# Convolution items, late gate operations and the split of w_out given lower scheduling rank in a hybrid encoder layer

## The chip, the core and the metric

The kernel runs on one core of one Trainium2 chip. The metric is the device time of one execution, in microseconds, as the median of several runs. The engines are TensorE (PE, with its weight loads shown as PEld), VectorE (DVE), ScalarE (ACT), GpSimd (POOL) and SyncE (SP), which issues the DMA transfers. Each engine executes its own list of instructions strictly in order, and waits on semaphores of the others.

## The reference

One layer of a hybrid encoder is applied to two requests with shared weights: a prompt of 512 tokens and a sample of 1024 tokens, model width 1024.

```python
h = rmsnorm(x, norm_attn_g);  z = h @ w_in
q, k, v, ca, cb = split(z)                     # 512, 128, 128, 512, 512 columns
a_out = window_attn(q, k, v, bias, sink)       # 8 heads of 64, 2 kv heads, |q-k| <= 128
c = ca * sigmoid(cb)
c = dwconv(c, conv_dw_w, 31 taps) + conv_dw_b
c = silu(layernorm(c, conv_ln_g, conv_ln_b))
x = x + concat(a_out, c) @ w_out
h = rmsnorm(x, norm_ffn_g)
u = dwconv(h @ w_up, ffn_dw_w, 3 taps) + ffn_dw_b   # 2 x 2816 columns
x = x + (silu(u[:, :2816]) * u[:, 2816:]) @ w_down
y = rmsnorm(x, norm_final_g)
```

All of it is float32.

## The kernel before

**Arithmetic.** A float32 product is emulated by three matmuls in the faster fp32r type. `split()` makes the two halves of an operand: the high half is a cast on ACT (L189), the low half is the subtraction of that cast from the original, on POOL or DVE (L190). A product of a 128-row chunk is then high x high, high x low, low x high, into one PSUM bank.

**Stages.** Work is cut into blocks of 128 tokens: blocks 0 to 3 are the prompt, 4 to 11 the sample.
1. The input projection (L296 to L299 in `proj()`), the prompt's attention and its output projection, to about 393 us.
2. The prompt's FFN up-projection in `ffn_step(k)`, 22 steps. A step makes a gate half and a value half with `up_half()`: 24 matmuls by `proj()` into a PSUM bank `u`, then the evacuation of the bank by ACT (L841) into a tile of the SBUF class `h`, with two taps of the 3-tap convolution read from the same bank by DVE (L837). The bank is free after the taps. `gate()` then makes tanh on ACT into a bank `b` (L861), two products on DVE and POOL (L866, L867), and the store of the result to DRAM (`gt`, L868). Beside these steps run the sample's attention (units 8 to 23, one for each block and kv head: `scores()`, then `values()`) and the sample's 31-tap convolution (`conv_items()`), whose result goes through DRAM (`cvd`).
3. The sample's output projection, from about 683 to 788 us. For each block `conv_norm()` loads the convolution's rows (L669), transposes them on PE (L675), makes the layer norm's statistics on DVE (L678, L681), transposes back (L687), applies scale and bias on ACT (four L690), tanh (L692), a product on DVE (L693) and a cast on ACT (L694). `out_half()` multiplies: matmuls L711, L712 and L713, 24 for each half block, of which the first twelve read the attention's rows and the last twelve the convolution's. Beside it run `pair_sums()` over the stored gates (on POOL, stores L883) and the first transposes of the sample's FFN input (`turned()`, L987).
4. The sample's FFN, whose order of instructions is written out by hand (the place `manual_schedule` in the program), to the end at 1557 us.

**The end of an attention unit.** `values()` ends with a copy of the result to a tile of class `h` (L638), a cast (L639), a subtraction on DVE (L640) and, on POOL, the sum L642 that frees both tiles.

**What sets the order.** In stages 1 to 3 the program is written once, in a certain order, and a scheduler lists the instructions of each engine: it plays the program through with estimated times, and among instructions that are ready takes the one with the lowest priority number (`tc.cur_priority`, which counts up as the program is written). So an instruction with a raised number yields to those that are written later, as long as they are ready. The place in the writing is set by three queues. `side` holds the generators of attention, w_out's split and conv_norm, and `tick()`, which `proj()` and `up_mm()` call as they go, advances it by `pace["rate"]` (RD in the FFN steps, RN after the attention). `convs` and `late` hold the generators of the convolution for the prompt and the sample. SBUF tiles come from fixed classes of slots (`q`, `c`, `h`, `d`, `s`; `h` has 61 slots of 2048 bytes per partition), handed out in the program by the class `Slots`; a tile that gets a used slot waits for the last reader of the tile before. PSUM banks are `a` (3), `u` (2), `b` (2) and `c` (1).

**w_out's split.** After attention unit 23, `sample()` goes through 16 + WOA pieces: each loads a piece of w_out (1024 rows as 8 x 128, in two halves of 512 columns) and, five pieces later, splits one (L189, L190).

Of the kernel before, what the change touches and what calls it, by code (L numbers as in the profile page):

```python
# [36 lines left out]

RA, RB, RBO, RD, RN, RE = 1.2, 0.8, 2.5, 0.8, 0.95, 0.9  # L40


CA, CB = 0.9, 0.4
# [10 lines left out]
OB = "uc"  # L54
VG = 3
NW = 36
KEEP = 3
U0 = 2


# [82 lines left out]
def tile_hybrid_encoder(ctx: ExitStack, tc: tile.TileContext, xs, rel_bias, norm_attn_g, w_in,  # L143
# [9 lines left out]

    sb = Slots(big, dict(q=(15, 4096), c=(4, 4224), h=(61, 2048), d=(2, 2176), s=(32, 64)), "q", KEEP)
    banks = Slots(lambda tag: ps[two_of[tag]], dict(a=(3, 2048), u=(2, 2048), b=(2, 2048), c=(1, 2048)))
    use = dict(step="aub", turn="aub", conv="c", attn="au", norm="b", out="b", up="u", down="b")
# [4 lines left out]
    def bank(job):  # L161
        return banks.tile([NT], among=use[job])
# [51 lines left out]
    def rows_T(parts, out):  # L214
        r = sb.tile([P])
        n = 0
        for src, k in parts:
            nc.sync.dma_start(r[n:n + k, :], src)
            n += k
        pt = bank("step")  # L220
        nc.tensor.transpose(pt[:, :n], r[:n, :], ident[:n, :n])
        nc.vector.tensor_copy(out, pt[:, :n])
# [3 lines left out]
    rows_T([(rw(norm_attn_g), 8)], vecs[:, 0:8])  # L226
    for _ in range(NW // 4):
        pt = bank("step")
# [36 lines left out]
    side, pace = deque(), dict(rate=0.0, due=0.0, conv=0.0, credit=0.0, late=0.0)  # L265

    def advance(queue):
        try:
            return next(queue[0])
        except StopIteration:  # L270
            queue.popleft()
            return 0.0
# [15 lines left out]
    def drain(queue):  # L288
        while queue:
            advance(queue)  # L290
# [21 lines left out]

    convs, late = deque(), deque()

    def conv_items(g, c, cp):
        T = GR[g]["T"]
        w = lambda t: cvw[:, t * 4 + c:t * 4 + c + 1]
        cost = 0.13 + NT / 960.0
        noff = NOFF[g]
        off = list(range(CK - noff, CK))  # L320
        for n in range(T // NT):
            src = lambda t: cp[:, t + n * NT:t + (n + 1) * NT]
            pacc = sb.tile([NT])

            def offload(k):
                t = off[k]
                if k == 0:
                    nc.scalar.activation(pacc[:], src(t), AF.Identity, scale=w(t))
                else:
                    pr = sb.tile([NT])  # L330
                    nc.scalar.activation(pr[:], src(t), AF.Identity, scale=w(t))
                    nc.gpsimd.tensor_tensor(pacc[:], pacc[:], pr[:], op=ALU.add)

            acc = bank("conv")
            nc.vector.tensor_scalar(acc[:], src(0), w(0), cvb[:, c:c + 1], op0=ALU.mult, op1=ALU.add)
            yield cost
            k = 0
            for t in range(1, CK - noff):
                nc.vector.scalar_tensor_tensor(acc[:], src(t), w(t), acc[:], op0=ALU.mult, op1=ALU.add)  # L339
                if t % 2 == 1 and k < noff:  # L340
                    offload(k)
                    k += 1
                yield cost
            while k < noff:
                offload(k)
                k += 1
            nc.vector.tensor_tensor(pacc[:], acc[:], pacc[:], op=ALU.add)
            del acc
            nc.sync.dma_start(cvd[g][:, c, n * NT:(n + 1) * NT], pacc[:])
            yield cost  # L350

    tanh_t, cpads, kt, vt = {}, {}, {}, {}
# [77 lines left out]
    def step(i, nt):  # L430
        kind, c, col = order[i]
        pp = bank("step")
        proj(pp[:], ws[i], h1[nt], i < 2 and nt == 0)
        evac(kind, c, nt, pp[:])
        if kind == "ca" and nt != 1:
            g = 0 if nt == 0 else 1
            (convs, late)[g].append(conv_items(g, c, cpads.pop((g, c))))
        tick()

    want_raw(1)  # L440
# [62 lines left out]
    bias = []  # L503
# [13 lines left out]
    qt, cats, units = {}, {}, {}  # L517
# [13 lines left out]
    score_rows = []  # L531

    def sink_columns():
        for h in range(0, NH, 2):
            t = sb.tile([2, NT])
            for n in range(2):
                nc.vector.tensor_copy(t[:, n, 0:1], nsink[:, h + n:h + n + 1])
            score_rows.append(t)
# [110 lines left out]
    def attention(u0, u1, then={}):  # L649
        yield from scores(u0)  # L650
        for u in range(u0, u1):
            if u + 1 < u1:
                yield from scores(u + 1)
            yield from values(u)
            if u in then:
                yield from then[u]
# [83 lines left out]
    def split_wo(kc, n, dve=False):  # L740
        wo[kc, n] = split(wor.pop((kc, n)), dve)
# [52 lines left out]
    def want_up_raw(k, half):  # L794
        if k < len(seq):
            upr[k, half] = chunk_raw(w_up[0], half * FF + seq[k][1] * P)
# [18 lines left out]
    def want_up(k, half):  # L815
        if k < len(seq):
            upw[k, half] = split(upr.pop((k, half)))
# [41 lines left out]
    def gate(j, a, b):  # L859
        th, t = bank("gate"), sb.tile([NT])  # L860
        nc.scalar.activation(th[:], a[:], AF.Tanh, scale=0.5)  # L861
        if j % 4 == VG:
            nc.vector.scalar_tensor_tensor(th[:], th[:], 1.0, a[:], op0=ALU.add, op1=ALU.mult)
            nc.vector.tensor_tensor(t[:], th[:], b[:], op=ALU.mult)
        else:
            nc.vector.scalar_tensor_tensor(t[:], th[:], 1.0, a[:], op0=ALU.add, op1=ALU.mult)  # L866
            nc.gpsimd.tensor_tensor(t[:], t[:], b[:], op=ALU.mult)  # L867
        nc.sync.dma_start(gt[j][:], t[:])  # L868
# [17 lines left out]
    def ffn_step(k):  # L886
        want_up_raw(k + 1, 1)
        ug = up_half(k, 0)
        want_up(k + 1, 0)
        uv = up_half(k, 1)  # L890
        want_up_raw(k + 2, 0)
        want_up(k + 1, 1)
        gate(k, ug[0], uv[0])

    use.update(attn="ab", gate="b")
    for half in range(2):
        want_up(0, half)
    want_up_raw(1, 0)
    load_bias()
    def sample():  # L900
        sink_columns()
        yield from attention(8, 24)
        kt.clear(), vt.clear(), qt.clear(), bias.clear(), score_rows.clear()
        use.update(norm="a")
        pace.update(rate=RN)
        for m in range(16 + WOA):
            if m in (10, 12):
                load_cat(m // 2 - 1)
            if m < 16:
                load_wo(m // 2, m % 2)  # L910
            if m >= WOA:
                split_wo((m - WOA) // 2, m % 2, m % 4 < DW2)
                yield 0.0
        drain(late)
        for m in range(NE):
            yield from conv_norm(4 + m)

    pace.update(rate=RD, late=CD)
    for k in range(NJ):
        if k == U0:  # L920
            side.append(sample())
        ffn_step(k)
# [320 lines left out]
    for j in range(2):  # L1243
        st[j] = dict(x=wide())
        prod(st[j]["x"][:, L], j, 1, True, True)
        a = sb.tile([NT])
# [322 lines left out]
    u, e, o11, o12 = (acc.pop(n) for n in ("u", "e", "o11", "o12"))  # L1569
# [73 lines left out]
```

## Time and profile before

| | |
|---|---|
| runs | 1566.2, 1563.84, 1559.77 us; median 1563.84 |
| profiled execution | 1558.91 us, its span 1557.1 us, granted clock 0.99 |
| PE busy | 1506.9 us (97%), 6843 instructions |
| DVE, ACT, POOL busy | 1126.2 (72%), 795.4 (51%), 708.9 us (46%) |
| DMA | 227.17 MB, mean 146 GB/s |
| 0 to 393 us | PE busy 367.0 of 393.0 us |
| 393 to 683 us (prompt's FFN, sample's attention) | PE busy 285.67 of 290.00 us |
| 683 to 788 us (sample's output projection) | PE busy 99.93 of 105.00 us |
| 788 us to the end (sample's FFN) | PE busy 754.29 of 769.00 us |

Starts and durations in the timeline's rows are in microseconds. A row names the engine, the line of the program, the operation, the tile written and the tiles read, and behind them in brackets how long the engine was idle just before, with the instruction whose end released it. Matmuls are pipelined, so their busy times overlap and the distance of two starts says how fast they go. The column PEclk is the clock granted to PE, as a share of the full one.

### The profile page before, as it was taken

The numbers are of one execution on the slowest core, as the hardware profiler recorded it, in microseconds if no ns is written. First come the engines' busy times: TensorE is split into PE (matmuls) and PEld (weight loads), VectorE is DVE, ScalarE is ACT, GpSimd is POOL, SyncE is SP. The second block draws the span as 40 slices with busy tenths as digits, with TensorE's granted clock in tenths as the row PEclk, the third lists the DMA queues.
The fourth block names the chain that finished last, engine by engine and source line by source line (L and its number), as shares of the span: only waits on it lengthen the run. The fifth ranks groups of instructions, "written<-read, shape, count | busy, mean of one in ns | idle before, by whom it ended". The sixth has DMA issues, their size and how long they took to land. (4 is left out here: it accounts for less than half of the span.)

```text
span 1557.1 us, 20112 instructions
## 1 busy us (share of the span) xinstructions
PE 1506.9 (97%) x6843; PEld 1229.4 (79%) x6843; DVE 1126.2 (72%) x1604; ACT 795.4 (51%) x1404; POOL 708.9 (46%) x566
## 2 busy tenths in 40 slices
PE   8899998999999999899999999999999999999997
PEld 6787787787888888777777888888888788888885
DVE  7999767857788785344868777777776845568883
ACT  4634654335787786633454444455545543444254
POOL 7652344226666776947433455555554000003355
PEclk9999999999999999999999999999999999999999
DMA  7582334447343346779332233333331582356644
GB/s 230 156 212 81 107 100 124 129 142 217 112 132 129 118 129 181 242 238 298 114 93 76 92 104 104 105 104 102 102 115 64 200 284 82 105 165 230 221 135 162
DMA packets 228780, 227.17 MB, mean 146 GB/s; under 512 B 13268, under 2 KB 168348, under 8 KB 228549
## 3 DMA queue, kind: packets, MB, share of 16 engines
q1 hardware_dynamic: 228677, 225.88, 45.8%
q8 instruction: 54, 0.88, 0.2%
q14 instruction: 49, 0.40, 0.1%
HBM read 164.74 MB, written 62.14 MB: 146 GB/s over the span
## 5 line engine op out<-in xcount | busy, mean ns | idle before, releaser
L190 POOL TENSOR_TENSOR q<-q,q 128x1024 fp32r<-128x1024 f32 x72 | 173.4, 2415 | 93.4 <-ACT q L189 34.4
L940 POOL TENSOR_TENSOR q<-q,q 128x512 fp32r<-128x512 f32 x101 | 140.0, 1391 | 164.0 <-ACT q L1050 151.7
L940 DVE TENSOR_TENSOR h<-h,h 128x512 fp32r<-128x512 f32 (+2 forms) x202 | 153.9, 794 | 65.2 <-ACT h L944 25.3
L1398 PE MATMUL w<-h,h 128*128 128x512 f32 x462 | 181.4, 393 | 1.4 <-DVE q L1185 1.4
L1399 PE MATMUL w<-h,h 128*128 128x512 f32 x462 | 181.5, 393 | 0.0
L1400 PE MATMUL w<-h,h 128*128 128x512 f32 x462 | 181.1, 392 | 0.0
L1064 PE MATMUL w<-h,q 128*128 128x512 f32 x448 | 176.5, 394 | 1.0 <-ACT h L1147 0.6
L1066 PE MATMUL w<-h,q 128*128 128x512 f32 x448 | 175.5, 392 | 1.0 <-POOL q L940 1.0
L1065 PE MATMUL w<-h,q 128*128 128x512 f32 x426 | 166.4, 391 | 0.0
L296 PE MATMUL u<-h,q 128*128 128x512 f32 x400 | 161.0, 403 | 5.4 <-DVE h L837 4.1
L297 PE MATMUL u<-h,q 128*128 128x512 f32 x400 | 158.6, 397 | 0.0
L299 PE MATMUL u<-h,q 128*128 128x512 f32 x384 | 151.8, 395 | 2.7 <-POOL q L190 2.7
L937 POOL TENSOR_TENSOR q<-q,q 128x1024 f32<-128x1024 f32 x12 | 32.4, 2707 | 236.6 <-DVE q L937 220.0
L339 DVE SCALAR_TENSOR_TENSOR c<-c,cvw,c 128x512 f32<-128x512 f32 x184 | 138.0, 750 | 2.9
L944 ACT CAST h<-h 128x512 fp32r<-128x512 f32 x120 | 71.9, 619 | 93.2 <-DVE h L940 41.9
L296 PE MATMUL b<-h,q 128*128 128x512 f32 x256 | 102.7, 401 | 3.3 <-DVE d L369 2.2
L1398 PEld LDWEIGHTS w<-h,h 128*128 128x128 f32 x462 | 86.8, 188 | 21.6 <-ACT h L944 1.8
L1400 PEld LDWEIGHTS w<-h,h 128*128 128x128 f32 x462 | 86.7, 188 | 19.7
L1399 PEld LDWEIGHTS w<-h,h 128*128 128x128 f32 x462 | 86.8, 188 | 19.5
L837 DVE SCALAR_TENSOR_TENSOR h<-u,fw,h 128x511 f32<-128x511 f32 x88 | 65.5, 744 | 49.8 <-ACT h L841 49.0
L299 PE MATMUL b<-h,q 128*128 128x512 f32 x256 | 101.4, 396 | 0.0
L297 PE MATMUL b<-h,q 128*128 128x512 f32 x256 | 101.1, 395 | 0.0
(417 smaller groups left out, 3670.4 us busy)
## 6 DMA issues: line engine op xcount, KB each, us to landing
q<-in_w_up SPq DMA_DIRECT2D x88, 512.0 KB
ga<-q SPq DMA_DIRECT2D x64, 256.0 KB
h<-ga SPq DMA_DIRECT2D x57, 256.0 KB
q<-in_w_in SPq DMA_DIRECT2D x28, 512.0 KB
h<-in_w_down SPq DMA_DIRECT2D x52, 256.0 KB
q<-in_x_sample SPq DMA_DIRECT2D x15, 512.0 KB
h<-qsd SPq DMA_DIRECT2D x24, 256.0 KB
x1d<-q SPq DMA_DIRECT2D x11, 512.0 KB
```

What stands on the lines that cost most here:

```text
L190: (nc.vector if dve else nc.gpsimd).tensor_tensor(lo[:], raw[:], hi[:].bitcast(F32), op=ALU.subtract)
L296: nc.tensor.matmul(out, whi[:, kc, :], hi[:], start=(kc == 0), stop=False)
L297: nc.tensor.matmul(out, whi[:, kc, :], lo[:], start=False, stop=False)
L299: nc.tensor.matmul(out, wlo[:, kc, :], hi[:], start=False, stop=(kc == KC - 1))
L339: nc.vector.scalar_tensor_tensor(acc[:], src(t), w(t), acc[:], op0=ALU.mult, op1=ALU.add)
L940: (eng or nc.vector).tensor_tensor(out, a, b, op=ALU.subtract)
L1064: nc.tensor.matmul(out, whi[:, s], hi[:], start=(start and c == 0), stop=False, **go)
L1065: nc.tensor.matmul(out, whi[:, s], lo[:], start=False, stop=False, **go)
L1066: nc.tensor.matmul(out, wlo[:, s], hi[:], start=False, stop=(stop and c == 3), **go)
L1398: nc.tensor.matmul(out, sh[:, c], th[:], start=(p == 0), stop=False)
L1399: nc.tensor.matmul(out, sh[:, c], tl[:], start=False, stop=False)
L1400: nc.tensor.matmul(out, sl[:, c], th[:], start=False, stop=(p == NPAIR - 1))
```

## The change

Five edits, none of which adds or removes an instruction; the number of instructions of each engine is the same as before.

1. RD, the pace of the side queue in the FFN steps, goes from 0.8 to 0.84, and RN, its pace after the attention, from 0.95 to 0.9.
2. A new wrapper `behind(gen, n)` raises the priority number by n while a generator writes its instructions. The convolution's generators get +200 (prompt) and +1500 (sample).
3. The instructions of `gate()` get +60.
4. The pieces of w_out become a generator of their own, `wo_pieces()`, with +150.
5. Two of these pieces are written after each of the attention units 19 to 23, and what is left of them after the last unit, as before.

```diff
--- before.py
+++ after.py
@@ -37,7 +37,7 @@
 
 
 
-RA, RB, RBO, RD, RN, RE = 1.2, 0.8, 2.5, 0.8, 0.95, 0.9
+RA, RB, RBO, RD, RN, RE = 1.2, 0.8, 2.5, 0.84, 0.9, 0.9
 
 
 CA, CB = 0.9, 0.4
@@ -54,7 +54,12 @@
 OB = "uc"
 VG = 3
 NW = 36
+WOU = 19
 KEEP = 3
+
+
+BACK = (200, 1500)
+BACKW, BACKG = 150, 60
 U0 = 2
 
 
@@ -311,6 +316,18 @@
     rs2 = cst.tile([P, 12], F32, name="rs2")
 
     convs, late = deque(), deque()
+
+    def behind(gen, n):
+
+        while True:
+            tc.cur_priority += n
+            try:
+                cost = next(gen)
+            except StopIteration:
+                return
+            finally:
+                tc.cur_priority -= n
+            yield cost
 
     def conv_items(g, c, cp):
         T = GR[g]["T"]
@@ -434,7 +451,7 @@
         evac(kind, c, nt, pp[:])
         if kind == "ca" and nt != 1:
             g = 0 if nt == 0 else 1
-            (convs, late)[g].append(conv_items(g, c, cpads.pop((g, c))))
+            (convs, late)[g].append(behind(conv_items(g, c, cpads.pop((g, c))), BACK[g]))
         tick()
 
     want_raw(1)
@@ -890,19 +907,16 @@
         uv = up_half(k, 1)
         want_up_raw(k + 2, 0)
         want_up(k + 1, 1)
+        tc.cur_priority += BACKG
         gate(k, ug[0], uv[0])
+        tc.cur_priority -= BACKG
 
     use.update(attn="ab", gate="b")
     for half in range(2):
         want_up(0, half)
     want_up_raw(1, 0)
     load_bias()
-    def sample():
-        sink_columns()
-        yield from attention(8, 24)
-        kt.clear(), vt.clear(), qt.clear(), bias.clear(), score_rows.clear()
-        use.update(norm="a")
-        pace.update(rate=RN)
+    def wo_pieces():
         for m in range(16 + WOA):
             if m in (10, 12):
                 load_cat(m // 2 - 1)
@@ -911,6 +925,21 @@
             if m >= WOA:
                 split_wo((m - WOA) // 2, m % 2, m % 4 < DW2)
                 yield 0.0
+
+    def some(gen, n):
+        for _ in range(n):
+            if next(gen, None) is None:
+                return
+            yield 0.0
+
+    def sample():
+        sink_columns()
+        wos = behind(wo_pieces(), BACKW)
+        yield from attention(8, 24, {u: some(wos, 2) for u in range(WOU, 24)})
+        kt.clear(), vt.clear(), qt.clear(), bias.clear(), score_rows.clear()
+        use.update(norm="a")
+        pace.update(rate=RN)
+        yield from wos
         drain(late)
         for m in range(NE):
             yield from conv_norm(4 + m)
```

The lines behind the first edits are shifted in the new program: by 5 up to `tick()` (L189 becomes L194, L296 becomes L301), by 17 from `conv_items()` on (L638 becomes L655, L642 becomes L659, L675 becomes L692, L687 becomes L704, L711 to L713 become L728 to L730, L841 becomes L858, L861 becomes L878), and by 29 behind `sample()` (L987 becomes L1016). On every engine the order is the same in both programs up to 393 us, and PE's again from 788 us on. In between it differs in many places; three of them follow. In the rows a tile stands as class and slot, the running number of the tile, and the instruction that wrote it.

First place, ACT near the end of the attention (645 to 654 us before). Here u_362 and u_363 are the two banks of step 19, one for the gate half and one for the value half. Before:

```order
L638 COPY h53_978_6332<-b0_360_6315 64x512
L639 CAST h24_957_6202<-b0_360_6315 64x512
L189 CAST q1_1024_6502<-q5_985_6362 128x1024
L189 CAST q12_1004_6435<-q0_981_6350 128x1024
L189 CAST h33_1042_6576<-h22_1028_6521 128x512
L841 ACTIVATE h46_1003_6431<-u0_362_6364,vecs_84,fw_275 128x512
L189 CAST h41_1052_6627<-h17_1031_6533 128x512
L189 CAST h31_1035_6547<-h24_1014_6474 128x512
L861 ACTIVATE b1_364_6506<-h46_1003_6431 128x512
L189 CAST h2_1012_6464<-h0_990_6383 128x512
L841 ACTIVATE h45_1022_6496<-u1_363_6439,vecs_84,fw_275 128x512
```

ACT of the change, from the evacuation of u_363 on, with the copy of the last attention unit (b0_360) in its middle:

```order
L635 CAST h40_1007_6388<-b1_358_6383 128x512
L858 ACTIVATE h19_1035_6522<-u1_363_6477,vecs_84,fw_275 128x512
L878 ACTIVATE b1_361_6418<-h32_996_6340 128x512
L655 COPY h32_1017_6449<-b0_360_6407 64x512
L656 CAST h48_982_6266<-b0_360_6407 64x512
L194 CAST q9_1023_6473<-q10_1012_6412 128x1024
L194 CAST h48_1020_6465<-h46_965_6180 128x512
L858 ACTIVATE h40_1022_6469<-u0_362_6426,vecs_84,fw_275 128x512
L878 ACTIVATE b1_364_6532<-h40_1022_6469 128x512
```

The evacuation of u_363 now stands ahead of that of u_362, and the latter, into slot h40, behind the copy of the last attention unit. The same place on POOL of the change, where slot h40 is read by the unit's last sum:

```order
L195 TENSOR_TENSOR h44_1006_6374<-h40_897_5788,h41_1005_6373 128x512
L195 TENSOR_TENSOR q1_1049_6582<-q3_1036_6526,q6_1048_6581 128x1024
L884 TENSOR_TENSOR q12_1015_6419<-q12_1015_6419,q9_1011_6408 128x512
L659 TENSOR_TENSOR h47_983_6267<-h40_1018_6450,h32_1017_6449 64x512
L195 TENSOR_TENSOR q0_1024_6474<-q10_1012_6412,q9_1023_6473 128x1024
```

The tile h40_1018 is the subtraction's result of the last unit, and h40_1022 of the rows above takes its slot.

Second place, PE in the output projection, block 6. The tile a_376 is the transpose of the block's convolution rows, a_377 the transpose back. Before:

```order
L675 MATMUL a2_376_6773<-ident_75,h56_1079_6767 128x128 x4
L711 MATMUL c0_375_6758<-h27_1032_6535,h24_1054_6637 128x512
L712 MATMUL c0_375_6758<-h58_1033_6536,h24_1054_6637 128x512
L711 MATMUL u0_378_6835<-h19_1029_6523,h24_1054_6637 128x512
L712 MATMUL u0_378_6835<-h16_1030_6524,h24_1054_6637 128x512
L713 MATMUL c0_375_6758<-h27_1032_6535,h4_1055_6638 128x512
```

PE of the change:

```order
L692 MATMUL a0_376_6773<-ident_75,h16_1079_6767 128x128 x4
L1016 MATMUL b0_392_7321<-ident_75,q12_1133_7042 128x128
L1016 MATMUL b1_393_7336<-ident_75,q12_1133_7042 128x128
L704 MATMUL a1_377_6793<-ident_75,h15_1085_6785 128x128 x4
L692 MATMUL a1_384_7061<-ident_75,h18_1137_7055 128x128 x4
L728 MATMUL u0_383_7046<-h49_1026_6486,h19_1077_6765 128x512
L729 MATMUL u0_383_7046<-h50_1027_6487,h19_1077_6765 128x512
L728 MATMUL u1_386_7123<-h48_1020_6465,h19_1077_6765 128x512
L729 MATMUL u1_386_7123<-h32_1021_6466,h19_1077_6765 128x512
```

Before, output matmuls of block 5 follow the transpose L675, and the transpose back stands 32 PE instructions later; in the change two single transposes stand between the two, and behind the transpose back one more transpose ahead of the matmuls that read the block's convolution rows (h19_1077). On SP, the load of block 6's convolution rows stands 11 instructions behind block 5's before, and 40 behind it in the change, after the loads and stores of the pair sums.

Third place, PE in block 7 of the change; a_381 and a_385 are the transposes back of blocks 7 and 8, c_387 is an output bank of block 7:

```order
L704 MATMUL a0_381_6934<-ident_75,h8_1112_6926 128x128 x4
L704 MATMUL a2_385_7081<-ident_75,h38_1143_7073 128x128 x4
L730 MATMUL u1_391_7308<-h26_971_6198,h47_1139_7058 128x512
L728 MATMUL u1_391_7308<-h41_1005_6373,h10_1138_7057 128x512
L729 MATMUL u1_391_7308<-h44_1006_6374,h10_1138_7057 128x512
L730 MATMUL u1_391_7308<-h41_1005_6373,h47_1139_7058 128x512
L1016 MATMUL b0_392_7321<-ident_75,q9_1160_7183 128x128
L1016 MATMUL b1_393_7336<-ident_75,q9_1160_7183 128x128
L728 MATMUL c0_387_7187<-h49_1026_6486,h16_1104_6906 128x512
```

Before, the transpose back of block 8 stands among the matmuls of c_387 that read attention rows (h10_1111, h12_1112), and the first with convolution rows (h9_1108) follows them:

```order
L711 MATMUL c0_387_7187<-h47_1001_6427,h10_1111_6916 128x512
L687 MATMUL a1_385_7081<-ident_75,h24_1143_7073 128x128 x4
L712 MATMUL c0_387_7187<-h1_1002_6428,h10_1111_6916 128x512
L713 MATMUL c0_387_7187<-h47_1001_6427,h12_1112_6917 128x512
L711 MATMUL c0_387_7187<-h2_1012_6464,h10_1111_6916 128x512
L712 MATMUL c0_387_7187<-h25_1013_6465,h10_1111_6916 128x512
L713 MATMUL c0_387_7187<-h2_1012_6464,h12_1112_6917 128x512
L711 MATMUL c0_387_7187<-h26_1020_6492,h10_1111_6916 128x512
L712 MATMUL c0_387_7187<-h28_1021_6493,h10_1111_6916 128x512
L713 MATMUL c0_387_7187<-h26_1020_6492,h12_1112_6917 128x512
L711 MATMUL c0_387_7187<-h27_1032_6535,h9_1108_6912 128x512
```

The transposes back of the two blocks now follow each other directly, and eight instructions behind the first stands the first matmul of c_387 with the convolution rows of block 7 (h16_1104).

## The prediction

> **What bounds the kernel now.** I read the page first, then the busy time by stage, then TensorE's timeline in the stages where it is not full, and last the other engines' timelines at the same moments.
>
> ```profile
> span 1557.1 us, 20112 instructions
> PE 1506.9 (97%) x6843; PEld 1229.4 (79%) x6843; DVE 1126.2 (72%) x1604; ACT 795.4 (51%) x1404; POOL 708.9 (46%) x566
> ```
>
> TensorE (PE) is the bound: 50 us of the span are left without a matmul. The change moves no matmul in or out, so the time can move only by what PE waits and by the clock that it is granted after a wait. Up to 393 us and from 788 us on, PE's order is the same in both programs; between them stand the 22 steps of the prompt's FFN with the sample's attention, and the sample's output projection.
>
> ```profile
> 393.00:640.00 247.00, 247.00 (x1199) 206.84 (x1198) 190.00 (x372) 188.59 (x358) 170.98 (x106) 1.00 0.45 141
> 640.00:655.00 15.00, 11.66 (x50) 8.93 (x48) 5.29 (x8) 10.66 (x17) 14.84 (x10) 1.00 0.86 268
> 655.00:663.00 8.00, 7.25 (x25) 5.85 (x26) 1.29 (x2) 0.00 (x0) 8.00 (x7) 0.79 0.39 132
> 684.00:690.00 6.00, 5.05 (x17) 4.09 (x18) 4.79 (x8) 2.69 (x5) 5.83 (x9) 0.72 1.03 364
> 690.00:730.00 40.00, 40.00 (x188) 32.78 (x188) 16.91 (x25) 14.56 (x31) 29.47 (x45) 1.00 0.87 288
> 730.00:750.00 20.00, 16.87 (x82) 13.16 (x81) 10.77 (x15) 6.80 (x14) 10.75 (x15) 1.00 0.81 264
> ```
>
> Columns: stretch, length, then busy us (and count) of PE, PEld, DVE, ACT, POOL, then the clock. From 393 to 640 us PE is never idle. It loses time at three places only: 640 to 663, 682 to 690, and 730 to 750. What it loses there is the most that can be won, and the clock column (0.79, 0.72) says that a wait costs more than itself.
>
> ```profile
> 650.32 0.40 PE L711 MATMUL c<-h,h 128*128 128x512 f32 x1
> 650.55 0.40 PE L712 MATMUL c<-h,h 128*128 128x512 f32 x1
> 651.59 0.47 PE L296 MATMUL u<-h,q 128*128 128x512 f32 x1 [0.64 <-DVE h L837]
> 651.90 0.40 PE L297 MATMUL u<-h,q 128*128 128x512 f32 x1
> 655.75 0.76 PE L296 MATMUL u<-h,q 128*128 128x512 f32 x1 [3.45 <-DVE h L837]
> 656.31 0.63 PE L297 MATMUL u<-h,q 128*128 128x512 f32 x1
> ...
> 658.87 0.41 PE L297 MATMUL u<-h,q 128*128 128x512 f32 x1
> ...
> 682.16 0.60 PE L675 MATMUL a<-ident,h 128*128 128x128 f32 x4
> 684.95 0.47 PE L711 MATMUL u<-h,h 128*128 128x512 f32 x1 [2.19 <-DVE s L678]
> ...
> 686.56 0.63 PE L711 MATMUL u<-h,h 128*128 128x512 f32 x1
> ...
> 689.12 0.85 PE L675 MATMUL a<-ident,h 128*128 128x128 f32 x4
> ```
>
> ```profile
> 734.11 0.66 PE L675 MATMUL a<-ident,h 128*128 128x128 f32 x4 [1.45 <-DMA h<-cvd]
> ...
> 744.29 0.44 PE L987 MATMUL b<-ident,q 128*128 128x128 f32 x2 [1.00 <-DVE q L958]
> ...
> 745.64 0.63 PE L687 MATMUL a<-ident,h 128*128 128x128 f32 x4 [0.67 <-DVE h L681]
> ```
>
> Starts are the clean measure, because matmuls overlap: at full clock one starts each 0.23 us (656.31 less 655.75 is already slow; 650.55 follows its neighbour by 0.23). First place: 1.04 - 0.23 = 0.81, then 3.85 - 0.23 = 3.62, then seven matmuls from 655.75 to 658.87 in 3.12 instead of 1.61, so 1.5: 5.9 us. Second: 2.79 less four transposes of 0.11 is 2.35, and six matmuls from 686.56 to 689.12 cost 2.56 instead of 1.38, so 1.2: 3.5 us. Third: 1.45 + 1.00 + 0.67 idle, by starts some 0.17 more each: 3.6 us. **13.0 us** in all.
>
> The first place is what the change speaks of. ACT takes its instructions in order:
>
> ```profile
> 651.70 0.62 ACT L189 CAST h<-h 128x512 fp32r<-128x512 f32 x1 [1.32 <-DMA h<-in_w_out]
> ...
> 653.26 0.77 ACT L841 ACTIVATE h<-u,vecs,fw 128x512 f32<-128x512 f32 x1
> 654.07 1.53 DVE L837 SCALAR_TENSOR_TENSOR h<-u,fw,h 128x511 f32<-128x511 f32 x2 [0.52 <-ACT h L841]
> 657.39 8.79 POOL L190 TENSOR_TENSOR h<-h,h 128x512 fp32r<-128x512 f32 x7
> ```
>
> The cast of a late w_out piece (L189) stands ahead of the evacuation of an FFN bank (L841); the taps (L837) follow, and only then may PE write the bank again at 655.75. POOL does w_out's low halves (1.26 us each) without a break until 666.
>
> **The change, part by part.** *Rates* (RD 0.84, RN 0.9) and *conv_items behind all else*: no instruction more or less; they shift units of the attention and the taps of the convolution against the FFN. In 393 to 640 DVE, ACT and POOL have 57, 58 and 76 us free, which hides any such shift; where the cover is gone, a late L837 costs PE one for one. I take 0, bounds -0.5 and +3 (TensorE was never idle there, so there is next to nothing to win).
>
> *The gate 60 later*: L861 to L868 come later; their results are read only after the FFN, so the delay itself is hidden. But the gate's inputs stay in SBUF longer, and the next step's tiles wait for slots. And its stores (L868) stand on SP ahead of loads of w_up.
>
> *w_out's split*: 48 loads on SP, 16 splits (0.62 on ACT, 1.26 on POOL each: 10 and 20 us) start some three FFN steps earlier. They are hidden behind PE there, by the same free time. What I then looked for is what comes last at the three places. With the casts spread, the wait at 655.75 for a w_out piece goes: -5.9. The order gives it a successor: the bank of u_362 (step 19's gate half) is evacuated behind the second half's bank and behind the last matmuls of the last attention unit, because its tile h40 is freed by that unit's last POOL sum (the order's L659, L642 before). The chain from the unit's last matmul to PE's next FFN matmul (u_365, same bank) is, from rows:
>
> ```profile
> 643.44 0.58 ACT L638 COPY h<-b 64x512 f32<-64x512 f32 x1
> 644.04 0.58 ACT L639 CAST h<-b 64x512 fp32r<-64x512 f32 x1
> ...
> 649.10 0.78 ACT L841 ACTIVATE h<-u,vecs,fw 128x512 f32<-128x512 f32 x1
> ```
>
> ```profile
> 644.65 0.69 DVE L640 TENSOR_TENSOR h<-b,h 64x512 f32<-64x512 f32 x1 [1.20 <-ACT h L639]
> 649.91 1.53 DVE L837 SCALAR_TENSOR_TENSOR h<-u,fw,h 128x511 f32<-128x511 f32 x2 [4.56 <-ACT h L841]
> ```
>
> ```profile
> 637.82 1.29 POOL L642 TENSOR_TENSOR h<-h,h 64x512 fp32r<-64x512 f32 x1
> ```
>
> L638 to the end of L640: 1.90 (643.44 to 645.34). L642: 1.29. L841 to the end of both L837: 2.34 (649.10 to 651.44). Sum 5.5, with three hand-overs of about 0.1 and 0.2 from PE to ACT 6.0. L638 also writes a tile (h32) that the gate of the step before reads last (L866, on DVE behind L841 and an L837 of the other bank): at most 0.9 more. PE has nothing else in its queue. I take 6.5 (6.0 to 6.9), plus 1.5 for the clock as at 655.75: **8.0** in place of 5.9.
>
> The second wait (684.95) goes: L841 of the last FFN bank now ends before the first `out` matmul needs the bank: -3.5. The third place changes most. SP's load of block 6's convolution (L669) stands 40 SP instructions behind block 5's, instead of 11, behind the pair sums' loads and stores. PE therefore does every `out` matmul that needs no conv rows first, and then stands in front of bare chains: transposes L675, statistics, transposes L687, activations, first matmul of the conv half. Their price is in the trace, where the prompt's blocks had them bare:
>
> ```profile
> 271.69 1.12 PE L687 MATMUL u<-ident,q 128*128 128x128 f32 x4 [4.03 <-DVE q L681]
> ...
> 276.61 1.09 PE L687 MATMUL u<-ident,h 128*128 128x128 f32 x4 [2.94 <-DVE h L681]
> ```
>
> ```profile
> 272.85 1.50 ACT L690 ACTIVATE h<-u,vecs 128x128 f32<-128x128 f32 x4 [2.23 <-PE u L687]
> 274.38 0.63 ACT L692 ACTIVATE q<-h 128x512 f32<-128x512 f32 x1
> 275.77 0.62 ACT L694 CAST h<-q 128x512 fp32r<-128x512 f32 x1 [0.76 <-DVE q L693]
> ```
>
> ```profile
> 275.05 0.69 DVE L693 SCALAR_TENSOR_TENSOR q<-q,h 128x512 f32<-128x512 f32 x1 [0.43 <-ACT q L692]
> ```
>
> L675 to L687 was bare for 2.94 and 4.03. In block 6 two transposes of 0.11 stand between: 2.7 to 3.8; I take 2.9, since DVE and ACT have no FFN work left. L687 to the end of L694: 272.85 to 276.39 and the hand-over, 3.6. Four transposes (0.44) stand between, which themselves wait for L690 to free their bank: 3.1 to 3.6, I take 3.4. With one slow stretch of 1.4 block 6 costs **7.7** (5.8 to 10.2). In block 7, ACT does block 8's four L690 (1.50) before block 7's L692: 5.1 behind L687, of which PE fills 0.44 + 4 x 0.23 + 0.22 = 1.6: 3.5, and 1.4 for the clock: **4.9** (3.0 to 5.0). The three waits of 730 to 750 have their loads much earlier than PE comes now: -3.6. Block 5's rows (L958 behind POOL's pair sums) come just in time: 0 to 2.4, I take **0.5**.
>
> Sum: 8.0 + 7.7 + 4.9 + 0.5 = 21.1 new against 13.0 gone: **+8.1 us**. On the profiled execution (1558.91, its span 1557.1) that gives 1567.0. That execution lies 4.9 below the median of the runs shown, 1563.84; the forecast goes by the median: 1572. The ends of the terms give +1.8 (6.0 + 5.8 + 3.0 less 13.0, no clock at the first) and +13.0 (8.4 + 10.2 + 5.0 + 2.4 less 13.0).
>
> On the clock: after a wait of 3.45 matmuls took 0.63, and so they did after one of 2.19, though not after 1.45. [...]
>
> **The rivals.** *The loads come late too* (slower still). The order puts a raw w_up load (q_1016, step 20's value half) on SP behind a gate store and two cat stores that end with the same POOL sum. A load's price:
>
> ```profile
> 639.74 0.38 SPq L183 DMA_DIRECT2D q<-in_w_up  x1
> ...
> 646.55 2.00 ACT L189 CAST q<-q 128x1024 fp32r<-128x1024 f32 x2 [1.93 <-DMA q<-in_w_up]
> ```
>
> At worst 6.8 us from issue to cast. From the POOL sum, PE's own way to u_366's third matmul is 2.4 + 5.5 + 1.5 + 0.5 = 9.9; store and load, cast 1.0 and POOL's 2.4 need 7 to 13. Beyond 9.9 PE waits again: up to 3, with the clock 4.5. Time 1572 + 4.5 = 1576. Chance 0.20.
>
> *The tile is freed in time* (no change). If the last unit's sums run before u_363 is through, the bank is free and the 8.0 fall away: 13.1 new against 13.0 gone, 1564. The order speaks against it: the unit's matmuls stand behind u_363 on PE. Chance 0.13.
>
> *The bare chains are short* (faster). Place: blocks 6 and 7. If ACT, DVE and POOL, idle by then, let both chains run behind PE's backlog, B and C together lose under 5, and with the tile freed in time the rest is nothing: it decides from new losses below 5.2 on, and gives 1563.84 - 13.0 + 5.0 = 1556. Against it: the parts alone (1.50 + 0.63 + 0.69 + 0.62) are 3.4 without a wait. Chance 0.08.
>
> **How the numbers follow.** A measurement of this kernel tells a change from none at about 0.5%, 7.8 us: 1556.0 to 1571.7. My forecast (0.59) lies at +8.1, on that edge: 0.31 of it above, 0.28 below. Slower: 0.31 + 0.20 = 0.51; same: 0.28 + 0.13 = 0.41; faster 0.08. Range: from the lower ends (+1.8 on the median, less the 4 us by which single runs lie below it) 1561, to the late loads with upper ends, 1581. It leaves out the fast rival and a little at the top.
>
> **What would show it.** Right: PE idle 6 to 7 us before an FFN matmul near 653 to 660 ended by L837 (the order's L854), idle 2 to 4 before an L687 and again before an L711 near 710 to 718, another near 735, and clock under 0.9 in these stretches; no wait for in_w_out on ACT near 650. Wrong: PE waiting between 393 and 640, or a span under 1560 with none of these waits. The forecast fails first if the FFN's bank is not held by h40.

## The result and the profile after

The changed kernel took 1582.8 us in the median (four runs, 1581.8 to 1587.8) against 1563.9 before: ratio 1.0129, 95% interval 1.0106 to 1.0152. It is slower by 18.9 us, on the side forecast, but over twice the 8.1 us of the forecast and 1.8 us above the range's upper end of 1581. The profiled execution took 1582.81, its span 1581.0.

```profile
span 1581.0 us, 20144 instructions
PE 1515.2 (96%) x6843; PEld 1235.9 (78%) x6843; DVE 1130.4 (71%) x1604; ACT 795.5 (50%) x1404; POOL 712.3 (45%) x566
```

The busy time by stage of the changed kernel, with the columns as above (stretch, length, busy us and count of PE, PEld, DVE, ACT, POOL, granted clock, then the share of the DMA engines and GB/s):

```profile
394.00:640.00 246.00, 246.00 (x1194) 205.51 (x1193) 188.90 (x370) 187.45 (x359) 174.18 (x108) 1.00 0.47 145
640.00:660.00 20.00, 14.87 (x67) 11.74 (x65) 6.17 (x9) 10.44 (x16) 15.64 (x11) 0.97 0.53 169
660.00:674.00 14.00, 10.68 (x35) 8.61 (x36) 4.21 (x6) 4.86 (x7) 7.62 (x5) 0.68 0.43 140
696.00:710.00 14.00, 9.65 (x45) 7.43 (x43) 4.72 (x6) 3.68 (x8) 8.70 (x12) 1.00 0.95 308
710.00:720.00 10.00, 9.76 (x37) 7.87 (x37) 1.61 (x3) 1.66 (x3) 6.20 (x10) 0.83 1.07 369
720.00:730.00 10.00, 4.55 (x23) 3.13 (x22) 4.52 (x8) 2.75 (x6) 5.66 (x9) 0.85 0.91 284
730.00:745.00 15.00, 15.00 (x60) 12.08 (x61) 5.85 (x8) 1.15 (x2) 7.60 (x14) 0.87 0.66 211
745.00:755.00 10.00, 6.59 (x28) 5.12 (x27) 3.40 (x5) 5.67 (x13) 6.40 (x7) 0.83 0.54 169
```

As before, PE is never idle up to 640 us: the moved casts and taps cost nothing there. Behind it stand four places of waiting, in TensorE's timeline:

```profile
663.32 0.77 PE L301 MATMUL u<-h,q 128*128 128x512 f32 x1 [8.46 <-DVE h L854]
663.89 0.63 PE L302 MATMUL u<-h,q 128*128 128x512 f32 x1
...
709.12 0.47 PE L728 MATMUL u<-h,h 128*128 128x512 f32 x1 [4.35 <-DVE q L987]
...
722.80 0.44 PE L1016 MATMUL b<-ident,q 128*128 128x128 f32 x2 [0.70 <-DVE q L987]
725.47 0.63 PE L704 MATMUL a<-ident,h 128*128 128x128 f32 x4 [2.23 <-DVE h L698]
727.69 1.12 PE L692 MATMUL a<-ident,h 128*128 128x128 f32 x4 [1.60 <-ACT h L707]
729.72 0.80 PE L728 MATMUL u<-h,h 128*128 128x512 f32 x1 [0.92 <-ACT h L711]
...
750.72 0.62 PE L728 MATMUL c<-h,h 128*128 128x512 f32 x1 [3.41 <-ACT h L711]
```

Three of them are the forecast's (u_365 at 663, block 6 at 723 to 730, block 7 at 751). The fourth, at 709, it had at 0.5 us. For sizes I took the distance of successive PE starts less the usual distance of that shape (0.23 us for 512 columns, 0.11 for a transpose of 128): "wait" where PE was idle before the start, "clock" the rest.

| place | forecast, wait + clock | measured, wait + clock |
|---|---|---|
| bank of u_362, 663 us | 6.5 + 1.5 | 8.6 + 2.8 |
| block 6's attention rows, 709 us | 0.5 | 4.9 + 1.6 |
| block 6's bare chain, 723 to 730 us | 6.3 + 1.4 | 6.2 + 2.6 |
| block 7, 751 us | 3.5 + 1.4 | 3.6 + 1.8 |
| waits of before that go | -13.0 | -14.0 |
| sum | +8.1 | +18.1 |

From the first PE instruction at which the orders differ to the last, PE needed 412.99 us instead of 394.88: the same 18.1. The rest of the 23.9 between the two spans lies where PE's order is the same (1.5 ahead of 393 us, the rest behind 788); that execution of before also lay 5 us below its median.

### The profile page after: what moved, and what is told of

The parts are those of the page before. It is cut to its first block, busy times and chain, and to the rows that moved or that the text cites. A ratio compares the mean times of both kernels' runs of the same rounds, so it can differ in the third digit from the quotient of the medians.

```text
span 1581.0 us, 20144 instructions
## 1 busy us (share of the span) xinstructions
PE 1515.2 (96%) x6843; PEld 1235.9 (78%) x6843; DVE 1130.4 (71%) x1604; ACT 795.5 (50%) x1404; POOL 712.3 (45%) x566
## 5 line engine op out<-in xcount | busy, mean ns | idle before, releaser
L195 POOL TENSOR_TENSOR q<-q,q 128x1024 fp32r<-128x1024 f32 x71 | 170.9, 2412 | 95.8 <-ACT q L194 38.6
L301 PE MATMUL u<-h,q 128*128 128x512 f32 x400 | 161.4, 404 | 9.3 <-DVE h L854 8.5
L301 PE MATMUL b<-h,q 128*128 128x512 f32 x256 | 102.8, 402 | 2.4 <-DVE d L386 1.7
L1093 PEld LDWEIGHTS w<-h,q 128*128 128x128 f32 x448 | 84.7, 189 | 23.4 <-ACT w L1185 2.5
```

The source lines that it names most:

```text
L195: (nc.vector if dve else nc.gpsimd).tensor_tensor(lo[:], raw[:], hi[:].bitcast(F32), op=ALU.subtract)
L301: nc.tensor.matmul(out, whi[:, kc, :], hi[:], start=(kc == 0), stop=False)
L1093: nc.tensor.matmul(out, whi[:, s], hi[:], start=(start and c == 0), stop=False, **go)
```

## The experiments

**First, which part.** Each engine's list of instructions in a built kernel says that three of the five edits do nothing by themselves. The change without the convolution's ranks, or without w_out's rank, has the same list on every engine, wait by wait; and each of the three ranks alone, at the old paces, gives the list of before. These were not run. Left are the paces, the spread, and the gate's rank together with them.

Paces alone: RD 0.84 and RN 0.9, everything else as before.

```diff
-RA, RB, RBO, RD, RN, RE = 1.2, 0.8, 2.5, 0.8, 0.95, 0.9
+RA, RB, RBO, RD, RN, RE = 1.2, 0.8, 2.5, 0.84, 0.9, 0.9
```

> The kernel before with RD 0.84 and RN 0.9 alone, no ranks and no spread. Theory 1 (the paces make the loss, since they shift the loads of the convolution's rows on SP: block 6's load stands 52 instructions behind block 5's in the order of this kernel, 11 before, 40 in the whole change): slower than before by 10 to 20 us, 1574 to 1584, with waits of PE of 2 to 4 us before the transposes back of blocks 6 to 8. Theory 2 (the spread of w_out's split makes the loss): within 5 us of before.

Measured 1585.5 (1.0141, interval 1.0119 to 1.0162), before in this group 1562.9. This is theory 1, and 1.5 us above its range.

The spread alone: ranks 0, old paces, WOU = 19.

> The kernel before with two pieces of w_out's split after each of the attention units 19 to 23 alone, paces as before. Block 6's load of the convolution's rows stands right behind block 5's on SP here. Theory 1: the wait for a late w_out piece near 655 us goes and no bare chain comes in its place, 1556 to 1566. Theory 2: slower than before by 10 us or more, 1574 or above, with PE waiting for an FFN bank near 650 to 660 us.

Measured 1564.95 (1.0011, 0.9998 to 1.0024). Theory 1 for the time. But a bare chain did come, at blocks 4 and 5, in place of what was won (PE's timeline of this kernel):

```profile
688.76 0.63 PE L692 MATMUL a<-ident,h 128*128 128x128 f32 x4 [2.19 <-DMA h<-cvd]
690.38 1.00 PE L704 MATMUL a<-ident,h 128*128 128x128 f32 x4 [1.00 <-DVE h L698]
692.99 1.12 PE L692 MATMUL a<-ident,h 128*128 128x128 f32 x4 [1.60 <-ACT h L707]
696.34 0.77 PE L728 MATMUL u<-h,h 128*128 128x512 f32 x1 [2.24 <-ACT h L711]
```

RD alone (0.84, RN 0.95), and RN alone (0.8, 0.9):

> The kernel before with RD 0.84 alone. Block 6's load stands 32 instructions behind block 5's on SP. Theory 1 in the form that RD does it: 1571 to 1582, nearly all of what both paces cost together. Rival: RN does it, and this kernel is within 4 us of before.

> The kernel before with RN 0.9 alone. Block 6's load stands 12 instructions behind block 5's on SP, as good as before. Theory 1 in the form that RD does it: 1560 to 1568, within 4 us of before. Rival: RN does it, 1571 or above.

Measured 1584.1 (1.0130, 1.0107 to 1.0153) and 1567.6 (1.0026, 1.0014 to 1.0038). RD makes the loss, and outdid the expectation's upper end of 1582.

The gate's rank taken out of the change (BACKG = 0):

> The whole change without the 60 on the gate. Block 6's load of convolution rows stands at place 387 on SP (379 in the change), PE's order differs in 24 rows. Theory (the gate's rank decides nothing, the slots do): 1578 to 1588. Rival (the gate's rank keeps slots and stores late): 1575 or below.

Measured 1589.4 (1.0175, 1.0151 to 1.0199): just above the theory's 1588. (Block 6's load stands at place 392 in this list; the 387 of the expectation is block 8's.) The rank does not make the loss; the interval just touches that of the change (1.0106 to 1.0152) from above, so if anything it saved a little.

**Second, why a pace of 5% costs so much.** In the lists the slow kernels had something in common: the tile of block 6's convolution rows lies in the slot that the product of the last gate (step 21) leaves. Its load then follows that product's store. SP's timeline of the changed kernel, with the store (L885) and the load (L686):

```profile
706.61 0.49 SPq L885 DMA_DIRECT2D gt<-h  x1
...
712.47 1.30 SPq L686 DMA_DIRECT2D h<-cvd  x2
```

Two further values of RD, with the rest of the change:

```diff
-RA, RB, RBO, RD, RN, RE = 1.2, 0.8, 2.5, 0.84, 0.9, 0.9
+RA, RB, RBO, RD, RN, RE = 1.2, 0.8, 2.5, 0.82, 0.9, 0.9
```

> The whole change, but RD 0.82 instead of 0.84. Block 6's convolution tile takes slot h56 here, and step 21's gate tile slot d0; its load stands 10 instructions behind block 5's on SP. Theory of slots (the loss after 700 us comes from block 6's convolution rows lying in the slot that the last gate's product leaves late, which at 0.84 is h16 for both): no bare chain before 730 us and 1560 to 1568. Rival (a faster side queue costs in proportion): half of the loss, 1570 to 1577.

> The whole change, but RD 0.88. Block 6's convolution tile takes slot h37 here, the one of step 21's gate tile; its load stands 30 instructions behind block 5's on SP. Theory of slots: slow again, 1574 to 1592, with PE idle over 2 us before the transpose back of block 6. Rival (0.84 is an unlucky value of its own): 1558 to 1570.

Measured 1567.5 at 0.82 (1.0025, 1.0012 to 1.0038) and 1592.6 at 0.88 (1.0187, 1.0167 to 1.0207), the latter 0.6 over the expected range, since PE also waited 10.5 us before 653 us there. PE's timeline at 0.88, at block 6's transpose back:

```profile
737.10 0.66 PE L704 MATMUL a<-ident,h 128*128 128x128 f32 x2 [5.82 <-DVE h L698]
```

And RD back at 0.8 in the change:

> The whole change with RD back at 0.8. Theory (RD makes the loss, by which tiles share which slots): 1561 to 1569, no wait of over 3 us between 700 and 760 us. Rival (RD loses only together with nothing else; the spread at the old pace loses as much in this setting): 1575 or above.

Measured 1569.2 (1.0028, 1.0015 to 1.0041), at the upper edge of the theory: the chain at blocks 4 and 5 of the spread alone is there again (8.8 us of waits and 4.6 of clock from 670 to 704 us). All kernels so far, with the slots as the lists have them:

| kernel | RD | slot of gate 21's product | slot of block 6's conv rows | its load behind block 5's on SP | us |
|---|---|---|---|---|---|
| before | 0.8 | h55 | h56 | 11 | 1563.9 |
| spread alone | 0.8 | h26 | h56 | 1 | 1565.0 |
| RN alone | 0.8 | h48 | h56 | 12 | 1567.6 |
| change, old RD | 0.8 | h19 | h56 | 1 | 1569.2 |
| change, RD 0.82 | 0.82 | d0 | h56 | 9 | 1567.5 |
| RD alone | 0.84 | h28 | h28 | 32 | 1584.1 |
| paces alone | 0.84 | h22 | h22 | 52 | 1585.5 |
| change | 0.84 | h16 | h16 | 40 | 1582.8 |
| change, gate not ranked | 0.84 | h16 | h16 | 52 | 1589.4 |
| change, RD 0.88 | 0.88 | h37 | h37 | 30 | 1592.6 |

(At 0.82 the distance is 9, where the expectation has 10.) That the slot is shared and that the kernel is slow go together in all ten rows. To show a cause, slots were then moved by hand.

**Third, slots moved by hand in the changed kernel.** The product of gate 21 elsewhere:

```diff
-        th, t = bank("gate"), sb.tile([NT])
+        th, t = bank("gate"), sb.tile([NT], among="d" if j == NJ - 1 else None)
```

> The whole change, with the product of the last gate (step 21) in a tile of class d instead of h. Everything behind takes the slot one earlier: block 6's attention rows are loaded 18 SP instructions earlier than in the change, block 6's convolution rows stay where they were (slot h23, which is late too). Theory (PE's wait at 709 us is for the load of block 6's attention rows): that wait of 4.5 us and its clock go, the waits near 723 to 730 and 751 stay, 1574 to 1579. Rival (it is the scaled row of block 4, behind POOL's pair sums, that PE waits for at 709 us): the wait stays, 1580 to 1585.

Measured 1583.2 (1.0122, 1.0102 to 1.0142). The wait at 709 shrank as the theory had it:

```profile
709.10 0.50 PE L730 MATMUL u<-h,h 128*128 128x512 f32 x1 [0.78 <-DMA h<-catd]
...
711.98 0.44 PE L1016 MATMUL b<-ident,q 128*128 128x128 f32 x2 [0.29 <-DVE q L987]
...
726.73 0.44 PE L1016 MATMUL b<-ident,q 128*128 128x128 f32 x2 [3.25 <-DVE q L987]
730.63 0.66 PE L704 MATMUL a<-ident,h 128*128 128x128 f32 x2 [3.46 <-DVE h L698]
```

But nothing was won: PE only came earlier to the bare chain and waited there for as much more (10.8 us at block 6 instead of 6.2). The time expected was wrong, since it let waits add up. And the kernel is slow with block 6's convolution rows in h23, another slot that comes late (place 380 on SP): so a slot that comes late is enough, and its owner need not be the gate.

The evacuation of u_362 elsewhere:

```diff
-            u = sb.tile([NT])
+            u = sb.tile([NT], among="d" if (k, half) == (19, 0) else None)
```

> The whole change, with the evacuation of bank u_362 (step 19, gate half) into a tile of class d instead of slot h40. On ACT it then stands ahead of the copy of the last attention unit. Theory (PE's wait of 8.5 us at 663 us is for slot h40, freed by the last unit's sum): that wait falls to 2 to 3 us, the halved clock behind it goes too, the later waits stay, 1572 to 1577. Rival (the load of the next w_up piece would hold PE anyway): the wait stays above 6 us, 1580 to 1585.

Measured 1585.5 (1.0151, 1.0127 to 1.0175). PE's timeline:

```profile
659.15 0.77 PE L301 MATMUL u<-h,q 128*128 128x512 f32 x1 [3.71 <-DVE d L854]
...
662.12 0.80 PE L304 MATMUL u<-h,q 128*128 128x512 f32 x1 [1.77 <-POOL q L195]
...
689.65 0.77 PE L728 MATMUL u<-h,h 128*128 128x512 f32 x1 [2.88 <-DVE h L854]
...
727.90 1.09 PE L704 MATMUL a<-ident,h 128*128 128x128 f32 x4 [5.24 <-DVE h L698]
```

The theory's wait shrank from 8.46 to 3.71, so slot h40 did hold the bank, by the place that it gave the evacuation on ACT. The time expected (1572 to 1577) was wrong again: w_up's split (L195), a new wait at 690 and a longer one at 728 took back what was won.

Block 6's convolution rows in class q, and its attention rows in class d:

```diff
-        cats[i, 0] = (sb.tile([4, P], F32R), sb.tile([4, P], F32R))
+        own = "d" if i == 6 else None
+        cats[i, 0] = (sb.tile([4, P], F32R, among=own), sb.tile([4, P], F32R, among=own))
...
-        cv = sb.tile([4, P])
+        cv = sb.tile([4, P], among="q" if i == 6 else None)
```

> The whole change, but block 6's convolution rows lie in a tile of class q and its attention rows in the two tiles of class d, none of them in a slot that an FFN step leaves late. On SP all three loads then stand ahead of the pair sums, and PE's order has the transposes of block 6 over 60 instructions apart. Theory of slots: the waits at 709 and at 723 to 730 us and their clock go (8.8 and 6.5 us together), the wait at 663 us stays, 1566 to 1574. Rival (the pair sums' transfers keep DMA and SP full, so that the wait only moves to the rows of blocks 7 and 8): 1578 or above.

Measured 1564.9 (1.0007, 0.9995 to 1.0019). This is the step that shows the cause: an edit that says only in which class of slots the tiles of one block lie takes back 17.9 of the 18.9 us, at the new paces, with the ranks and the spread. Later tiles are dealt other slots by it too: block 7's convolution rows get h7, and their load stands at place 345 on SP instead of 401. How much of the 17.9 us is block 7's is not shown. PE's timeline has the first wait nearly as in the change (7.16 us instead of 8.46), and only two more up to 790 us:

```profile
662.43 0.76 PE L301 MATMUL u<-h,q 128*128 128x512 f32 x1 [7.16 <-DVE h L855]
...
711.07 0.63 PE L705 MATMUL a<-ident,h 128*128 128x128 f32 x4 [1.79 <-DVE s L696]
...
719.77 0.49 PE L729 MATMUL u<-h,h 128*128 128x512 f32 x1 [3.22 <-ACT h L712]
```

Each half of that edit alone:

> The whole change, with block 6's convolution rows alone in a tile of class q. The slot that step 21's gate leaves (h16) then goes to the next asker, block 6's attention rows, whose load moves from place 366 to 386 on SP. Theory (whatever of block 6 lies in the late slot stops PE, so both kinds of rows have to be moved at once): the bare chain at 723 goes, but PE waits some 4 to 8 us for the attention rows instead, 1574 to 1584. Rival (the convolution rows alone make the loss after 700 us): 1564 to 1572.

> The whole change, with block 6's attention rows alone in the two tiles of class d. Theory: the wait at 709 us goes, but the convolution rows stay in h16 and come no earlier, so that PE reaches the bare chain sooner and waits there by as much more, as in the two kernels in which one wait alone was taken away: 1578 to 1586. Rival (the two waits add up, each is worth its own size): the 6.5 us of that wait are won, 1574 to 1578.

Measured 1572.0 (1.0050, 1.0032 to 1.0069) and 1581.9 (1.0113, 1.0093 to 1.0133). The convolution rows alone win 10.8 us, 2 better than the theory's range, 0.01 outside the rival's; the attention rows alone 0.9, which is not clear of noise. The sum of the two is 11.7, together they won 17.9. PE's timelines, of the first and of the second:

```profile
715.06 0.69 PE L1016 MATMUL b<-ident,q 128*128 128x128 f32 x2 [4.63 <-DVE q L987]
716.71 0.80 PE L728 MATMUL u<-h,h 128*128 128x512 f32 x1 [0.96 <-DMA h<-catd]
```

```profile
707.98 0.44 PE L1017 MATMUL b<-ident,q 128*128 128x128 f32 x2 [2.09 <-DVE q L988]
...
721.89 0.45 PE L1017 MATMUL b<-ident,q 128*128 128x128 f32 x2 [3.37 <-DVE q L988]
724.57 1.08 PE L705 MATMUL a<-ident,h 128*128 128x128 f32 x4 [2.22 <-DVE h L699]
```

With the convolution rows away, h16 went to the attention rows, as expected, but PE waited 0.96 us for their load and 4.63 for a scaled row (L987), so the theory's reason holds in part only. With the attention rows away the chain remained, and scaled rows (L988 there) held PE twice. Why these come in time only when both are moved was not followed further. The two halves also leave block 7's load late, at places 387 and 399, so part of the difference between 11.7 and 17.9 may be block 7's.

Both of block 6, and u_362's evacuation in class q as well:

> As the kernel with block 6's rows in own slots, and the evacuation of bank u_362 in a tile of class q as well. Theory of slots: the wait at 663 us falls by 5 to 6 us too and nothing takes its place, 1558 to 1568, the loss of the change gone. Rival (what is won early is waited for later, as when u_362 alone got its own slot): no faster than the kernel with block 6 alone, 1570 or above.

Measured 1566.1 (1.0013, 1.0000 to 1.0026). That lies in the theory's range and under the rival's 1570, but it is no faster than with block 6 alone (1564.9), as the rival had it. The waits speak for the rival too: the one at u_365 fell from 7.16 to 4.79, and a new one of 3.01 stood at the first output matmuls (694 us).

**Fourth, a faster version.** The spread without the new paces and the ranks, where block 5's rows had taken the slot of block 4's (h32), with the rows of both in class q, and then block 8's too:

```diff
-        cv = sb.tile([4, P])
+        cv = sb.tile([4, P], among="q" if i in (4, 5, 8) else None)
```

> The spread of w_out's split alone at the old paces, with the convolution rows of blocks 4 and 5 in tiles of class q (with the spread alone block 5's rows took the slot of block 4's, h32, and PE waited 8 us and 3 us of clock for bare chains at 689 to 697 us). Theory of slots: that loss goes and nothing else changes, 1551 to 1558, faster than before by about 0.5%. Rival: the wait moves to a later block, 1560 to 1566.

> As the kernel with the spread and own slots for the convolution rows of blocks 4 and 5, with block 8's rows in a tile of class q too. In that kernel PE still waited 4.4 us at 722 to 724, for the load of a later block's rows. Theory of slots: 1 to 4 us faster than it, 1551 to 1555. Rival (the wait moves on to blocks 9 to 11): 1555 to 1560.

Measured 1555.35 (0.9945, 0.9928 to 0.9962) and 1552.5 (0.9929, 0.9910 to 0.9947): faster than before and than the change, both inside the ranges of the theory of slots. The 2.9 us of the second step are not clear of noise, since the two intervals overlap. The busy time by stage of the last one:

```profile
640.00:690.00 50.00, 49.64 (x230) 40.26 (x230) 21.21 (x34) 22.65 (x38) 37.42 (x36) 1.00 0.66 220
690.00:710.00 20.00, 20.00 (x97) 16.36 (x96) 8.18 (x14) 7.15 (x15) 12.74 (x22) 1.00 1.01 333
710.00:740.00 30.00, 28.81 (x134) 22.72 (x133) 18.08 (x23) 10.03 (x20) 25.21 (x33) 1.00 0.91 301
```

From 640 to 740 us PE is idle for 1.6 us, and the granted clock is 1.00 throughout. The DMA engines are as full as in the changed kernel (share 0.91 to 1.01 from 690 to 740 us, there 0.85 to 1.07 from 690 to 730), so full DMA engines alone did not make the waits; what the moved tiles changed is which transfer comes first.

## Why the prediction was too small

**Right.** PE without a wait up to 640 us; no wait of PE for a late piece of w_out (ACT still waited 1.83 us for one at 646 us, but PE was busy); a successor at the same bank through h40 and the last unit's sum (shown by the kernel with u_362's evacuation moved); bare chains at blocks 6 and 7, 6.2 and 3.6 us against 6.3 and 3.5; slower. None of the rivals came: no load of w_up held PE between 664 and 709 us, the tile was not freed in time, and the chains were not short.

**The term of 0.5 for block 5's rows measured 6.5.** That step looked at one of the two inputs that PE needs there, the scaled rows behind POOL's pair sums, and found them nearly in time. It did not ask when SP would issue the load of block 6's attention rows. SP's, POOL's and DVE's timelines of the changed kernel:

```profile
703.95 0.97 SPq L678 DMA_DIRECT2D h<-catd  x2
...
705.99 0.56 SPq L678 DMA_DIRECT2D h<-catd  x1
```

```profile
705.01 0.72 POOL L896 TENSOR_TENSOR h<-h 128x256 f32<-128x256 f32 x1 [4.36 <-DMA h<-gt]
```

```profile
707.36 1.74 DVE L987 SCALAR_TENSOR_TENSOR q<-q,rs,q 128x1024 f32<-128x1024 f32 x1 [5.14 <-POOL rs L179]
```

PE was through at 704.8, and the load was issued 0.9 us ahead of that. The row of PE names the scaled rows (L987), which ended at 709.10, but in the built kernel's list this matmul waits for the load and for an evacuation on DVE that was done before 699. By the trace's record of semaphores the load's last piece landed at 708.99. L987 is needed two matmuls later, by the transposes at 709.66 (L1016). So both were late, and either alone would have held PE to about 709. With the load 18 places earlier 2.9 us of the 4.9 stayed (0.9 for the load of the rows' low half, 0.5 for a scaled row, 1.5 for a cast, L711), and with the load earliest of all PE still waited 2.09 for the scaled rows at 708.

**The clock was taken as one slow stretch of 1.4 to 1.5 for each place; the four measured 8.8 us against 4.3.** In the trace's record of the granted clock the slow stretches between 640 and 760 us, at 0.5 of the full clock, last 10.24, 3.41, 6.83 and 3.41 us, in before twice 3.41. The longest began in the middle of the one wait of 8.46 us and went on for 5.7 us behind it; the one of 6.83 belongs to the waits close together in block 6. PE loses 0.43 - 0.23 = 0.20 us with each matmul of 512 columns in such a stretch.

**The chain at u_365 was 2.1 us longer.** ACT and POOL of the changed kernel:

```profile
655.77 0.58 ACT L655 COPY h<-b 64x512 f32<-64x512 f32 x1 [0.98 <-DVE q L883]
656.36 0.58 ACT L656 CAST h<-b 64x512 fp32r<-64x512 f32 x1
657.05 1.04 ACT L194 CAST q<-q 128x1024 fp32r<-128x1024 f32 x1
660.19 0.62 ACT L194 CAST h<-h 128x512 fp32r<-128x512 f32 x1 [2.09 <-DMA catd<-h]
660.83 0.78 ACT L858 ACTIVATE h<-u,vecs,fw 128x512 f32<-128x512 f32 x1
```

```profile
657.87 1.26 POOL L659 TENSOR_TENSOR h<-h,h 64x512 fp32r<-64x512 f32 x1 [0.84 <-DVE h L657]
```

ACT waited 0.98 us for the gate's read of h32 (the forecast had 0.9 as its upper end and took half). Most of the rest is a row that the forecast passed over: ACT stood 2.09 us at a cast of w_out whose slot waited for the store of an attention tile to land, with the evacuation L858 behind it. The sum L659 had freed h40 at 659.13, and L858 started 1.70 us later. So a cast of w_out still stood in the way, though the change had spread them.

**What the forecast left out as a whole** is what moved the place of block 6's load. It took the load's place from the list and priced it, without asking what ties the load to the last gate. That tie, a slot, made the terms hang together: they were added as if each could be had alone, and in the runs they could not.

## What to carry to other kernels

Where tiles come from a fixed set of slots in the order of the writing, a small change of pace deals the slots anew, and a load can inherit a slot whose last owner is late; look for the pair (last reader of the slot, next load into it) at each place where a transfer stands late in its queue, before changing paces or ranks. Waits on one in-order engine do not add up: taking one away is worth only what the next one doesn't take back (here 10.8 and 0.9 us for the two halves of block 6, 17.9 for both). Moving one tile also deals later tiles new slots, so what such a move wins need not belong to that tile alone. A rank that changes no list costs and wins nothing, and the lists of a built kernel say so ahead of any run.

## What was not expected of the hardware

Whether a wait costs clock does not go by its length alone. In before, the wait of 2.19 us that ended at 684.95 was followed, from 686.56 on, by matmuls 0.43 us apart (granted clock 0.72 from 684 to 690 us). Another of 2.19 us, early in the same execution, was followed by matmuls 0.23 us apart (clock 1.00 from 48 to 62 us):

```profile
52.45 0.50 PE L296 MATMUL b<-h,q 128*128 128x512 f32 x1 [2.19 <-DVE d L369]
52.78 0.39 PE L297 MATMUL b<-h,q 128*128 128x512 f32 x1
53.01 0.40 PE L299 MATMUL b<-h,q 128*128 128x512 f32 x1
53.25 0.40 PE L296 MATMUL b<-h,q 128*128 128x512 f32 x1
```

A wait of 3.22 us (the kernel with block 6 moved) was followed, from 720.66 on, by matmuls 0.43 us apart (clock 0.94 from 710 to 740 us); one of 3.30 us (spread with blocks 4 and 5 moved) by matmuls 0.23 us apart, and there the granted clock is 1.00 in every stretch from 640 to 765 us. PE's timelines of the two:

```profile
720.33 0.53 PE L729 MATMUL u<-h,h 128*128 128x512 f32 x1
720.66 0.63 PE L730 MATMUL u<-h,h 128*128 128x512 f32 x1
721.08 0.63 PE L731 MATMUL u<-h,h 128*128 128x512 f32 x1
...
723.64 0.49 PE L731 MATMUL u<-h,h 128*128 128x512 f32 x1
```

```profile
721.95 0.66 PE L692 MATMUL a<-ident,h 128*128 128x128 f32 x4 [3.30 <-DMA h<-cvd]
722.36 0.47 PE L728 MATMUL c<-h,h 128*128 128x512 f32 x1
722.67 0.39 PE L729 MATMUL c<-h,h 128*128 128x512 f32 x1
722.90 0.39 PE L728 MATMUL u<-h,h 128*128 128x512 f32 x1
```

In the first, eight matmuls from 720.33 to 723.64 took 3.31 us instead of 8 x 0.23 = 1.84. So of two waits of nearly one length, in one execution each, one cost 1.5 us of clock and the other none. What decides between them was not shown.
